# A scan traced in sixteen steps with three pieces of the q, k and v projections each, its dependent products queued behind a piece, and state buffers for each direction

## The chip, the core and the metric

The kernel runs on one core of a Trainium2 chip. A core has a matrix engine (TensorE, PE in the profile), a vector engine (VectorE, DVE), an activation engine (ScalarE, ACT), a general engine (GpSimd, POOL) and a queue engine that issues most transfers (SyncE, SP). Each of them works through its own instructions in a fixed order and waits on semaphores for the others. The metric is the device time of one execution in microseconds (us), taken as the median of several runs.

## The reference

One layer of a hybrid encoder on 1024 tokens of width 1024, in float32. What matters here is its first half:

```python
h = rmsnorm(x, norm_mix_w)
z, xbc, dt_raw, q, k, v = jnp.split(h @ w_in, offs, axis=-1)
y_ssm = ssd_mixer(z, xbc, dt_raw, ...)
y_na = neighbourhood_attention(q, k, v, ...)
x = x + jnp.concatenate([y_ssm, y_na], axis=-1) @ w_out
h = rmsnorm(x, norm_mlp_w)
return x + jnp.square(jax.nn.relu(h @ w_mlp_in)) @ w_mlp_out
```

`ssd_mixer` is a scan with a state, run forward and backward over 8 chunks of 128 tokens, for 2 groups of 8 heads with 64 columns each. In each direction a chunk needs the state that the chunk before it left:

```python
cb = jnp.einsum("bclgn,bcsgn->bclsg", cc, bc)
y_diag = jnp.einsum("bclsge,bcsgep->bclgep", cb[..., None] * decay, xc)
chunk_states = jnp.einsum("bclgn,bclgep->bcgepn", bc, xc * decay_to_end[..., None])
def step(h, inp):
    s_c, d_c = inp
    return d_c[..., None, None] * h + s_c, h
y_off = jnp.einsum("bclgn,bcgepn->bclgep", cc, h_in) * jnp.exp(a_cum)[..., None]
```

The two directions are added, gated with SiLU(z), normalised in groups of 512 columns and handed to the output projection together with the attention's result.

## The kernel before

Every large product is made of float32 split into a high and a low part: `mm3` (L177 to L180) issues three products for each step of the contraction. The low part of a weight (tile wl) is what VectorE or GpSimd subtracts from the raw load (wraw), the high part (wh) is copied by ScalarE (L148, L149).

The program runs in stages: the norm and transposes of h (to about 50 us), the projections to x, B, C with the convolution and to z (to 264.8 us), then the scan together with the projections to q, k and v (264.8 to 671.2 us), attention with a part of the output projection, the rest of the output projection, and the two layers of the MLP. The change rewrites the scan and its projections.

A scheduler orders the instructions of each engine before the program runs: it simulates the engines by a model of its own and gives each engine, of what is ready, what was traced first. The order in which the source issues things is thus a priority, and where instructions end up is seen in the built program only.

Names of the scan, for direction d, chunk c and group g (a chunk's 128 tokens by 512 columns):

- xs: the inputs, loaded from DRAM (L585 backward, L670 forward). xw: xs weighted for the state (L653, L672), split into xh and xl (L540, L541).
- `decay_state`: pS is the chunk's part of the state (product L541 and following by `mm3`), st the running state (L546, L549, L550), sh and sl its split (L553, L554). The buffer of sh and sl is one for each group, shared by both directions.
- `carried`: py is the part of the output that the carried state makes (`mm3` with sh, sl as its operands), yo the scaled py (L567); ch, cl is the split of C (L562, L563).
- `backward` also makes the part within the chunk, for both directions together: pcb is B times C (L587), rb the decay weights (two loads of 512 KB, L605; GpSimd subtracts, L612; VectorE's predicated copy, L618; the exponential, L623; times pcb, L625), pd the product of rb and xs (L630, eight products), y1 the sum (L638 to L642). The forward output of the first half of the chunks and the backward output of the second half go to DRAM (y1_dr) and are fetched again by the other direction (L648, L665).
- `gated`: times SiLU(z) (tile sz), the norm, and the store to y_dr (L579), on the queue of ScalarE.
- PSUM: pcb, pS and py take turns in two buffers (`ps_s`), the transposes ptq in two (`ps_tp`), pd has its own, the projections pq have others.

The scan's loop runs over the chunks and groups, 16 steps, and calls backward(7 - i, g) and forward(i, g). After it the projections are traced: for each of two halves of the columns q, then k, then v, each in 8 pieces. A piece is 128 tokens by 512 columns, 24 products pq, and what follows it (norm, transposes ptq, split hl, store). There are 48 pieces. Being traced after the scan they have the lower priority and fill the holes that the scan leaves on TensorE.

Behind that stage stand attention (L852 and following: loads of q, k, kl and v for a pair of heads, the mask nam, L786, the bias braw, L876, their sum mb on GpSimd, L881, scores psc, L931 and L934, their row maximum with the masked scores pr, L939, transposes ptp, L962) and the output projection that fills its holes (yl: loads of the gated scan output, L798; pty: its transposes, L807; po: its products; x: the residual, L830).

Of the kernel before, what the change touches and what calls it, by code (L numbers as in the profile page):

```python
# [9 lines left out]
F32 = mybir.dt.float32  # L10
F32R = mybir.dt.float32r
# [7 lines left out]
P = 128  # L19
# [36 lines left out]
def hymba_block(  # L56
# [162 lines left out]
    with ExitStack() as ph:  # L219
# [298 lines left out]
        with ExitStack() as p2:  # L518
# [15 lines left out]

            def decay_state(d, c, g, xw):
                prev = st[d][g]
                pS = ps_s("pS")
                xh = qp.tile([P, 512], F32R, tag="xh", name="xh", bufs=1)
                xl = qp.tile([P, 512], F32R, tag="xl", name="xl", bufs=1)
                nc.scalar.activation(xh, xw, AF.Copy)  # L540
                nc.vector.tensor_tensor(xl, xw, xh.bitcast(F32), op=sub)  # L541
                mm3(pS, bNh[:, c, g, :], bNl[:, c, g, :], xh, xl, True, True)
                new = prev and prev[0]
                if prev is None:
                    new = qp.tile([P, 512], F32, tag=f"st{d}{g}", name="st", bufs=1)
                    nc.vector.tensor_copy(new, pS)  # L546
                else:
                    dec = ed[:, d, c, 8 * g : 8 * g + 8]
                    nc.gpsimd.tensor_tensor(h8(new), h8(new), hb(dec), op=mul)  # L549
                    nc.vector.tensor_tensor(new, new, pS, op=add)  # L550
# [3 lines left out]
                nc.vector.tensor_tensor(sl, new, sh.bitcast(F32), op=sub)  # L554
                st[d][g] = (new, sh, sl)
# [24 lines left out]

            def backward(c, g):
                hs = slice(8 * g, 8 * g + 8)
                cs = slice(c * P, (c + 1) * P)
                xs = qp.tile([P, 512], F32, tag="xs", name="xs")
                nc.sync.dma_start(xs, xs_dr[c, :, g * 512 : (g + 1) * 512])  # L585
                pcb = ps_s("pcb")
                nc.tensor.matmul(  # L587
                    pcb[:, 0:P], lhsT=bT[:, g, cs], rhs=cT[:, g, cs], start=True, stop=True
                )
                cb = pcb[:, 0:P]  # L590
                jk = pcb[:, P : 2 * P]
                cd = qp.tile([P, 1], F32, tag="cd", name="cd")
                nc.vector.scalar_tensor_tensor(
                    jk, cb, 1.0, ident, op0=mul, op1=mul, accum_out=cd
                )
                cf = qp.tile([P, 8], F32, tag="cf", name="cf")
                nc.vector.scalar_tensor_tensor(
                    cf, dt[:, 1, c, hs], cd, dsk[:, hs], op0=mul, op1=add
                )
                pd = ps_v("pd")  # L600
                for q in range(2):
# [9 lines left out]
                    for d in range(2):  # L611
# [11 lines left out]
                    nc.scalar.activation(rb[:, 0], rb[:, 0], AF.Exp)  # L623
                    gm = rb[:, 0]
                    nc.vector.tensor_tensor(  # L625
                        gm, rb[:, 0], cb.unsqueeze(1).broadcast_to([P, 4, P]), op=mul
                    )
                    for j in range(4):
                        e = 4 * q + j
                        nc.tensor.matmul(  # L630
                            pd[:, e * HD : (e + 1) * HD],
                            lhsT=gm[:, j, :],
                            rhs=xs[:, e * HD : (e + 1) * HD],
                            start=True,
                            stop=True,
                        )
                y1 = qp.tile([P, 512], F32, tag="y1", name="y1")
                nc.gpsimd.tensor_tensor(h8(y1), h8(xs), hb(cf), op=mul)  # L638
                if c < NT - 1:
                    yo = carried(1, c, g)  # L640
                    nc.gpsimd.tensor_tensor(y1, y1, yo, op=add)
                nc.vector.tensor_tensor(y1, y1, pd, op=add)  # L642
                if c >= NT // 2:
                    nc.scalar.dma_start(y1_dr[c, :, g * 512 : (g + 1) * 512], y1)
                else:
# [4 lines left out]
                    gated(y1, c, g)  # L650
                if c > 0:
                    xw = qp.tile([P, 512], F32, tag="xw", name="xw", bufs=1)
                    nc.gpsimd.tensor_tensor(h8(xw), h8(xs), hb(wd[:, 1, c, hs]), op=mul)  # L653
                    decay_state(1, c, g, xw)

            def forward(c, g):
                hs = slice(8 * g, 8 * g + 8)
# [10 lines left out]
                if c < NT - 1:  # L668
                    xs = qp.tile([P, 512], F32, tag="xs", name="xs")
                    nc.sync.dma_start(xs, xs_dr[c, :, gs])  # L670
                    xw = qp.tile([P, 512], F32, tag="xw", name="xw", bufs=1)
                    nc.gpsimd.tensor_tensor(h8(xw), h8(xs), hb(wd[:, 0, c, hs]), op=mul)  # L672
                    decay_state(0, c, g, xw)
# [35 lines left out]

            for g in range(2):  # L710
                ps4 = slice(4 * g, 4 * g + 4)
                for b, pt, rt in qkv_proj(OFF_Q, g):
                    hl = normed_split(pt, rt, pcol[:, 80:81])
                    s = slice(b * P, (b + 1) * P)
                    for j in range(2):
                        for a in range(2):
                            nc.scalar.dma_start(
                                q_dr[ps4, 2 * j + (a ^ j), :, s].rearrange("p d t -> d p t"),
                                hl[j * HD : (j + 1) * HD, a],
                            )  # L720
                for b, pt, rt in qkv_proj(OFF_K, g):
                    hl = normed_split(pt, rt, pcol[:, 81:82])
                    nc.scalar.dma_start(
                        k_dr[g, :, :, :, b * P : (b + 1) * P].rearrange(
                            "a p f t -> f (a p) t"
                        ),
                        hl.rearrange("f a p t -> f (a p) t"),
                    )
                for b, pt, rt in qkv_proj(OFF_V, g):
                    hl = hp.tile([P, 8, 2, HD], F32R, tag="hl", name="hl", bufs=2)  # L730
                    split_from_psum(hl[:, :, 0], hl[:, :, 1], h8(pt), rt)
                    nc.scalar.dma_start(v_dr[b, :, 8 * g : 8 * g + 8], hl.bitcast(F32))

# [655 lines left out]
```

## Time and profile before

| | us |
|---|---|
| three runs, median | 1681.8 |
| lowest and highest | 1676.36 and 1685.55 |
| span of the profiled execution | 1676.4 |
| scan with the q, k and v projections | 264.8 to 671.2 |

The profiled execution's span agrees with the fastest run. The time outside the span is not seen apart in this profile. An engine's busy time in the page is a sum of the lengths of its instructions; those of TensorE overlap. "PE pcb L587 <- DVE yo L567: 6.7, 4, 2.6" reads: TensorE stood before the product pcb of line 587, and what it waited for last was VectorE's instruction that makes yo at line 567; 6.7 us in total, in 4 waits, the longest 2.6 us. In a row of the timeline the first number is the start in us from the span's start, the second the length, and the brackets hold the idle time before it with its releaser.

### The profile page before, as it was taken

The page shows a single profiled execution, that of the slowest core. Times are in us where ns is not written, and L with a number is a line of the kernel's source. Part 1 is how long each engine was busy: PE and PEld are TensorE (multiplying, and loading weights), DVE is VectorE, ACT ScalarE, POOL GpSimd, SP SyncE. Part 2 cuts the span into 40 slices and gives each one's busy share as a digit, 9 for nine tenths or more (in the row PEclk, how much of TensorE's full clock was granted, in tenths as well). Part 3 has the DMA queues.
Part 4 walks back from the last instruction along what each step waited for, and adds up shares of the span by engine and source line. Part 5 has one row for each costly group of instructions (what it writes and reads, how often), then busy time and mean ns, then how long its engine had stood idle before and what let it go on. Part 6 is the DMA issues. An engine that isn't in the chain of part 4 may idle for free. (4 is left out here: it accounts for less than half of the span.)

```text
span 1676.4 us, 20931 instructions
## 1 busy us (share of the span) xinstructions
PE 1590.8 (95%) x7453; PEld 1297.3 (77%) x7453; DVE 1106.0 (66%) x1686; ACT 721.3 (43%) x1187; POOL 708.4 (42%) x506
## 2 busy tenths in 40 slices
PE   6999999998988899998999989999999989999999
PEld 5788888777766678887778767788888868888887
DVE  5767214788796852888898867544243387887863
ACT  5434223434343442556565533554444444433330
POOL 4000003888687862322243232244444465455551
PEclk9999999999999999999999999999999989999999
DMA  8113337876666785956664141353344386644231
GB/s 217 51 38 105 93 100 212 215 194 196 229 220 173 218 263 190 281 165 185 180 190 118 62 164 50 101 201 126 138 164 150 127 295 231 216 149 151 101 101 75
DMA packets 178755, 269.75 MB, mean 161 GB/s; under 512 B 14219, under 2 KB 105307, under 8 KB 178651
## 3 DMA queue, kind: packets, MB, share of 16 engines
q1 hardware_dynamic: 134667, 227.51, 44.1%
q10 hardware_dynamic: 42976, 37.23, 7.3%
q0 software_dynamic: 1008, 3.67, 0.5%
q8 instruction: 59, 0.97, 0.3%
q14 instruction: 45, 0.37, 0.1%
HBM read 185.21 MB, written 86.50 MB: 162 GB/s over the span
## 5 line engine op out<-in xcount | busy, mean ns | idle before, releaser
L760 POOL TENSOR_TENSOR wl<-wraw,wh 128x1024 fp32r<-128x1024 f32 x110 | 298.5, 2724 | 318.4 <-ACT wh L759 297.1
L759 ACT ACTIVATE wh<-wraw 128x1024 fp32r<-128x1024 f32 x110 | 115.6, 1054 | 149.7 <-PE px L745 50.8
L745 PE MATMUL px<-wh,ahl 128*128 128x512 f32 x512 | 162.5, 395 | 3.3 <-ACT ahl L759 3.3
L179 PE MATMUL pq<-wl,hTh 128*128 128x512 f32 x384 | 153.6, 402 | 4.9 <-DVE wl L149 4.8
L178 PE MATMUL pq<-wh,hTh 128*128 128x512 f32 x384 | 154.4, 405 | 3.5 <-ACT wh L148 3.5
L745 PE MATMUL px<-h,wh 128*128 128x512 f32 x496 | 156.0, 396 | 1.4 <-DVE x L1078 1.4
L180 PE MATMUL pq<-wh,hTl 128*128 128x512 f32 x384 | 152.9, 399 | 0.0
L760 DVE TENSOR_TENSOR ahl<-ar,ahl 128x1024 fp32r<-128x1024 f32 x56 | 115.1, 2062 | 23.2 <-ACT ahl L759 22.1
L759 ACT ACTIVATE ahl<-ar 128x1024 fp32r<-128x1024 f32 x56 | 58.2, 1052 | 140.1 <-PE px L745 75.3
L745 PEld LDWEIGHTS px<-wh,ahl 128*128 128x128 f32 x512 | 97.0, 190 | 25.0 <-ACT ahl L759 3.7
L745 PEld LDWEIGHTS px<-h,wh 128*128 128x128 f32 x496 | 93.2, 188 | 24.0 <-ACT h L184 1.6
L149 DVE TENSOR_TENSOR wl<-wraw,wh 128x1024 fp32r<-128x1024 f32 x40 | 55.3, 1386 | 81.9 <-ACT wh L148 81.2
L745 PE MATMUL px<-wl,ahl 128*128 128x512 f32 x256 | 101.0, 395 | 0.0
L745 PE MATMUL px<-h,wl 128*128 128x512 f32 x248 | 98.1, 395 | 0.0
L881 POOL TENSOR_TENSOR mb<-braw,nam 128x256 f32<-128x256 f32 (+1 forms) x48 | 40.1, 863 | 131.1 <-DVE nmx L939 72.2
L179 PEld LDWEIGHTS pq<-wl,hTh 128*128 128x128 f32 x384 | 73.6, 192 | 23.1 <-DVE wl L149 8.6
L149 POOL TENSOR_TENSOR wl<-wraw,wh 128x1024 fp32r<-128x1024 f32 x18 | 43.0, 2401 | 110.5 <-ACT wh L148 110.5
L178 PEld LDWEIGHTS pq<-wh,hTh 128*128 128x128 f32 x384 | 74.0, 193 | 20.2 <-ACT wh L148 5.2
L184 ACT ACTIVATE pth<-ptp 128x384 fp32r<-128x384 f32 (+1 forms) x128 | 57.7, 455 | 73.1 <-PE ptp L962 72.5
L612 POOL TENSOR_TENSOR rb<-rb,c 128x512 f32<-128x512 f32 x64 | 77.0, 1223 | 20.4 <-DMA rb<-cum_dr 19.2
L180 PEld LDWEIGHTS pq<-wh,hTl 128*128 128x128 f32 x384 | 73.5, 191 | 15.0
L745 PE MATMUL pz<-h,wh 128*128 128x512 f32 x256 | 80.8, 396 | 0.8 <-DVE h L185 0.8
(268 smaller groups left out, 4211.4 us busy)
## 6 DMA issues: line engine op xcount, KB each, us to landing
ar<-act_dr SPq DMA_DIRECT2D x56, 512.0 KB, 3.7
act_dr<-cq SPq DMA_DIRECT2D x49, 512.0 KB, 3.2
wraw<-in_w_in_dram SPq DMA_DIRECT2D x44, 512.0 KB, 4.3
rb<-cum_dr SPq DMA_DIRECT2D x32, 512.0 KB, 7.2
wraw<-in_w_mlp_in_dram SPq DMA_DIRECT2D x32, 512.0 KB, 4.6
wraw<-in_w_mlp_out_dram SPq DMA_DIRECT2D x32, 512.0 KB, 5.2
q_dr<-hl ACTq DMA_DIRECT2D x64, 128.0 KB, 3.6
k_dr<-hl ACTq DMA_DIRECT2D x16, 512.0 KB, 5.3
```

Source lines behind the costliest of these rows:

```text
L149: lo_eng.tensor_tensor(lo[:, 0:n], raw[:, 0:n], hi[:, 0:n].bitcast(F32), op=sub)
L178: nc.tensor.matmul(pt, lhsT=ah, rhs=bh, start=first, stop=False)
L179: nc.tensor.matmul(pt, lhsT=ah, rhs=bl, start=False, stop=False)
L180: return nc.tensor.matmul(pt, lhsT=al, rhs=bh, start=False, stop=last)
L184: nc.scalar.activation(hi, src, AF.Copy)
L612: nc.gpsimd.tensor_tensor(rb[:, d], rb[:, d], c1[:, d, c, h0 : h0 + 4].unsqueeze(2).broadcast_to([P, 4, P]), op=sub,)
L745: nc.tensor.matmul(pt, lhsT=a, rhs=b, start=f, stop=l, skip_group_check=True)
L759: nc.scalar.activation(hl[0], src, AF.Copy)
L760: eng.tensor_tensor(hl[1], src, hl[0].bitcast(F32), op=sub)
L881: nc.gpsimd.tensor_tensor(mb[:, s].rearrange("p (s r c) -> p s r c", r=16, c=8), v[:, a:b], nam[:, s].rearrange("p (s r c) -> p s r c", r= ...
```

## The change

The scan's step is taken apart. `weights(c, g)` does all that does not need this step's projections: the loads, the chain of rb as far as the product with pcb, pcb, and the carried output of the backward direction. Then the next piece of the projections is traced; `mark` is its last product. Then follow `backward`, whose state product pS and whose pd are put behind `mark` on TensorE (`tc.issue_after(mark)`), `forward` with the same mark for its pS, and two more pieces. One piece stands ahead of the loop. So each of the 16 steps has three pieces, in place of projections that are traced after the whole scan.

pcb moves from the two buffers that it shared with pS and py to the two of the transposes. xh and xl get two buffers each. sh and sl get a buffer for each direction and group. `dynamic_dma_scratch_size=4096` is set for the program, and the memory that this frees holds the additional buffers.

```diff
-            def decay_state(d, c, g, xw):
+            def decay_state(d, c, g, xw, mark):
                 prev = st[d][g]
                 pS = ps_s("pS")
-                xh = qp.tile([P, 512], F32R, tag="xh", name="xh", bufs=1)
-                xl = qp.tile([P, 512], F32R, tag="xl", name="xl", bufs=1)
+                xh = qp.tile([P, 512], F32R, tag="xh", name="xh", bufs=2)
+                xl = qp.tile([P, 512], F32R, tag="xl", name="xl", bufs=2)
...
-                mm3(pS, bNh[:, c, g, :], bNl[:, c, g, :], xh, xl, True, True)
+                with tc.issue_after(mark):
+                    mm3(pS, bNh[:, c, g, :], bNl[:, c, g, :], xh, xl, True, True)
...
-                sh = qp.tile([P, 512], F32R, tag=f"sh{g}", name="sh", bufs=1)
-                sl = qp.tile([P, 512], F32R, tag=f"sl{g}", name="sl", bufs=1)
+                sh = qp.tile([P, 512], F32R, tag=f"sh{d}{g}", name="sh", bufs=1)
+                sl = qp.tile([P, 512], F32R, tag=f"sl{d}{g}", name="sl", bufs=1)
...
-            def backward(c, g):
+            def weights(c, g):
...
-                pcb = ps_s("pcb")
...
+                    rbs.append(rb)
+                pcb = ps_tp("pcb")
...
+                for rb in rbs:
                     nc.vector.tensor_tensor(
...
+                if c < NT - 1:
+                    yo = carried(1, c, g)
+                    nc.gpsimd.tensor_tensor(y1, y1, yo, op=add)
+                return xs, rbs, y1
+
+            def backward(c, g, xs, rbs, y1, mark):
+                hs = slice(8 * g, 8 * g + 8)
+                if c > 0:
+                    xw = qp.tile([P, 512], F32, tag="xw", name="xw", bufs=1)
+                    nc.gpsimd.tensor_tensor(h8(xw), h8(xs), hb(wd[:, 1, c, hs]), op=mul)
+                    decay_state(1, c, g, xw, mark)
+                pd = ps_v("pd")
+                with tc.issue_after(mark):
+                    for e in range(8):
                         nc.tensor.matmul(
...
-            for i in range(NT):
-                for g in range(2):
-                    backward(NT - 1 - i, g)
-                    forward(i, g)
...
-                        mm3(pt, hTh[s], hTl[s], *get(k), k == 0, k == KD - 1)
-                    yield b, pt, rcol[:, b : b + 1]
+                        mark = mm3(pt, hTh[s], hTl[s], *get(k), k == 0, k == KD - 1)
+                    yield b, pt, rcol[:, b : b + 1], mark.ins
...
+            units = qkv_units()
+            mark = next(units)
+            for n in range(2 * NT):
+                c, g = n // 2, n % 2
+                held = weights(NT - 1 - c, g)
+                mark = next(units)
+                backward(NT - 1 - c, g, *held, mark)
+                forward(c, g, mark)
+                for _ in range(2):
+                    mark = next(units, mark)
+            for mark in units:
+                pass
...
+    nc = bacc.Bacc(
+        "TRN2", target_bir_lowering=False, num_devices=1, dynamic_dma_scratch_size=4096
+    )
```

`qkv_units` is the old loop over q, k and v with its stores, which now hands out its mark after each piece.

What this does to the order shows at three places. The first is TensorE in the middle of the scan. Before, pd, pS and py of a step stand in one block, and the projections' products behind and ahead of it:

```order
L178 MATMUL pq<-wh,hTh 128x512
L179 MATMUL pq<-wl,hTh 128x512
L630 MATMUL pd<-xs,rb 128x64 x8
L178 MATMUL pS<-xh,bNh 128x512
L179 MATMUL pS<-xl,bNh 128x512
L180 MATMUL pS<-xh,bNl 128x512
L178 MATMUL py<-sh,ch 128x512
L179 MATMUL py<-sl,ch 128x512
L180 MATMUL py<-sh,cl 128x512
L705 MATMUL ptq<-ident,qn 128x128 x8
L180 MATMUL pq<-wh,hTl 128x512
L178 MATMUL pq<-wh,hTh 128x512
```

In the changed program one step's pS and py are still neighbours, but pd stands apart, a few products of a piece behind them (line 646 is pd's, line 178 to 180 are the three products of `mm3`):

```order
L179 MATMUL pS<-xl,bNh 128x512
L180 MATMUL pS<-xh,bNl 128x512
L178 MATMUL py<-sh,ch 128x512
L179 MATMUL py<-sl,ch 128x512
L180 MATMUL py<-sh,cl 128x512
L178 MATMUL pq<-wh,hTh 128x512
L179 MATMUL pq<-wl,hTh 128x512
L180 MATMUL pq<-wh,hTl 128x512
L178 MATMUL pq<-wh,hTh 128x512
L179 MATMUL pq<-wl,hTh 128x512
L180 MATMUL pq<-wh,hTl 128x512
L646 MATMUL pd<-xs,rb 128x64 x4
```

So the dependent products come in smaller groups with pieces between; the step's pcb stands 40 rows ahead of that pd, with a whole piece in between.

The second place is TensorE at the end of the stage. Before, the first scores of attention stand among the products of the projections, with some 190 of these still to come:

```order
L178 MATMUL pq<-wh,hTh 128x512
L179 MATMUL pq<-wl,hTh 128x512
L180 MATMUL pq<-wh,hTl 128x512
L931 MATMUL psc<-k,q 128x256
L934 MATMUL psc<-kl,q 128x256
L178 MATMUL pq<-wh,hTh 128x512
L931 MATMUL psc<-k,q 128x384
L934 MATMUL psc<-kl,q 128x384
L179 MATMUL pq<-wl,hTh 128x512
```

In the changed program they stand behind the last projection product (the third row), and the transposes of the output projection's operand (pty) and its first products (po) follow:

```order
L178 MATMUL pq<-wh,hTh 128x512
L179 MATMUL pq<-wl,hTh 128x512
L180 MATMUL pq<-wh,hTl 128x512
L940 MATMUL psc<-k,q 128x256
L940 MATMUL psc<-k,q 128x384
L943 MATMUL psc<-kl,q 128x256
L943 MATMUL psc<-kl,q 128x384
L816 MATMUL pty<-ident,yl 128x128 x8
L178 MATMUL po<-wh,yh 128x512
L179 MATMUL po<-wl,yh 128x512
L178 MATMUL po<-wh,yh 128x512
L179 MATMUL po<-wl,yh 128x512
```

What moved is the scan's end towards the projections' end: in the changed order the last py of the scan has 24 projection products behind it, and the last pd 19.

The third place is the queue of SP there, which issues loads in order. Before (y is the last fetch of y1_dr, then the loads for the first pair of heads, the mask, the gated scan output and the bias; the residual x comes twelve issues later):

```order
L665 DMA y_3415<-y_dr 128x512
L852 DMA q<-q_dr 128x2x1024
L855 DMA k<-k_dr 64x2x1024 x2
L866 DMA kl<-k_dr 64x1024 x2
L868 DMA v<-v_dr 128x8x256
L786 DMA nam<-namask_dram 128x896
L798 DMA yl<-y_dr 128x8x128 x4
L876 DMA braw<-t_dr 128x384
```

In the changed program:

```order
L672 DMA y_5386<-y_dr 128x512
L861 DMA q<-q_dr 128x2x1024
L864 DMA k<-k_dr 64x2x1024 x2
L875 DMA kl<-k_dr 64x1024 x2
L877 DMA v<-v_dr 128x8x256
L147 DMA wraw<-in_w_out_dram 128x2x512 x2
L839 DMA x_5441<-in_x_dram 128x512 x7
L795 DMA nam<-namask_dram 128x896
L807 DMA yl<-y_dr 128x8x128 x4
L885 DMA braw<-t_dr 128x384
```

The loads of x, which take the memory of h and so wait for the last projection product, have moved ahead of nam, yl and braw.

More of the change, by code (lines that the diff above doesn't have):

```diff
@@ L585, in backward @@
                 nc.sync.dma_start(xs, xs_dr[c, :, g * 512 : (g + 1) * 512])
-                pcb = ps_s("pcb")
[L587 to L600, printed above, removed]
+                rbs = []
                 for q in range(2):
@@ L623, in backward @@
                     nc.scalar.activation(rb[:, 0], rb[:, 0], AF.Exp)
-                    gm = rb[:, 0]
+                    rbs.append(rb)
+                pcb = ps_tp("pcb")
+                nc.tensor.matmul(
+                    pcb[:, 0:P], lhsT=bT[:, g, cs], rhs=cT[:, g, cs], start=True, stop=True
+                )
+                cb = pcb[:, 0:P]
+                jk = pcb[:, P : 2 * P]
+                cd = qp.tile([P, 1], F32, tag="cd", name="cd")
+                nc.vector.scalar_tensor_tensor(
+                    jk, cb, 1.0, ident, op0=mul, op1=mul, accum_out=cd
+                )
+                cf = qp.tile([P, 8], F32, tag="cf", name="cf")
+                nc.vector.scalar_tensor_tensor(
+                    cf, dt[:, 1, c, hs], cd, dsk[:, hs], op0=mul, op1=add
+                )
+                y1 = qp.tile([P, 512], F32, tag="y1", name="y1")
+                nc.gpsimd.tensor_tensor(h8(y1), h8(xs), hb(cf), op=mul)
+                for rb in rbs:
                     nc.vector.tensor_tensor(
-                        gm, rb[:, 0], cb.unsqueeze(1).broadcast_to([P, 4, P]), op=mul
+                        rb[:, 0], rb[:, 0], cb.unsqueeze(1).broadcast_to([P, 4, P]), op=mul
                     )
-                    for j in range(4):
-                        e = 4 * q + j
+                if c < NT - 1:
[11 more added lines that the diff above has]
+                    for e in range(8):
                         nc.tensor.matmul(
                             pd[:, e * HD : (e + 1) * HD],
-                            lhsT=gm[:, j, :],
+                            lhsT=rbs[e // 4][:, 0, e % 4, :],
                             rhs=xs[:, e * HD : (e + 1) * HD],
@@ L708, in normed_split @@
                 return hl.bitcast(F32).rearrange("f a (p t) -> f a p t", p=4)
[L710 to L732, printed above, removed]
@@ new lines, in qkv_units @@
+            def qkv_units():
+                for g in range(2):
+                    ps4 = slice(4 * g, 4 * g + 4)
+                    for b, pt, rt, mark in qkv_proj(OFF_Q, g):
+                        hl = normed_split(pt, rt, pcol[:, 80:81])
+                        s = slice(b * P, (b + 1) * P)
+                        for j in range(2):
+                            for a in range(2):
+                                nc.scalar.dma_start(
+                                    q_dr[ps4, 2 * j + (a ^ j), :, s].rearrange("p d t -> d p t"),
+                                    hl[j * HD : (j + 1) * HD, a],
+                                )
+                        yield mark
+                    for b, pt, rt, mark in qkv_proj(OFF_K, g):
+                        hl = normed_split(pt, rt, pcol[:, 81:82])
+                        nc.scalar.dma_start(
+                            k_dr[g, :, :, :, b * P : (b + 1) * P].rearrange(
+                                "a p f t -> f (a p) t"
+                            ),
+                            hl.rearrange("f a p t -> f (a p) t"),
+                        )
+                        yield mark
+                    for b, pt, rt, mark in qkv_proj(OFF_V, g):
+                        hl = hp.tile([P, 8, 2, HD], F32R, tag="hl", name="hl", bufs=2)
+                        split_from_psum(hl[:, :, 0], hl[:, :, 1], h8(pt), rt)
+                        nc.scalar.dma_start(v_dr[b, :, 8 * g : 8 * g + 8], hl.bitcast(F32))
+                        yield mark
```

15 lines of the change are left out of this document (3 added, 12 removed).

## The prediction

> **What bounds the kernel now.** I read the page first, then the windows of the stage that the change rewrites (264.8 to 671.2 us, from the first to the last product of the q, k and v projections), then the waits of TensorE there, then single rows.
>
> ```profile
> PE 1590.8 (95%) x7453; PEld 1297.3 (77%) x7453; DVE 1106.0 (66%) x1686; ACT 721.3 (43%) x1187; POOL 708.4 (42%) x506
> 264.80:671.20 406.40, 371.29 (x1748) 297.62 (x1747) 290.87 (x419) 155.09 (x270) 285.39 (x266) 0.97 0.74 216
> 280.00:600.00 320.00, 287.23 (x1371) 228.73 (x1370) 258.91 (x375) 128.03 (x230) 253.97 (x235) 0.97 0.73 208
> 540.00:550.00 10.00, 5.95 (x21) 4.38 (x22) 8.06 (x13) 3.19 (x6) 9.84 (x9) 0.83 0.54 130
> 560.00:570.00 10.00, 7.89 (x31) 4.69 (x29) 9.55 (x10) 5.48 (x9) 8.87 (x7) 1.00 0.88 246
> 650.00:660.00 10.00, 10.00 (x46) 8.29 (x45) 1.50 (x2) 0.96 (x2) 0.00 (x0) 1.00 0.27 107
> ```
>
> Columns of the last five are the length, busy time of PE, PEld, DVE, ACT and POOL, the granted clock, the DMA share and GB/s. PE bounds the whole kernel, but this stage has two faces. While the scan runs (280 to 600) VectorE is busy 81% (258.91 of 320) and GpSimd 79% (253.97), and PE has holes. From about 600 on PE runs projection products alone, without a hole, and the vector engines idle. Those products start 0.23 us apart though each counts as 0.39 busy:
>
> ```profile
> L178 PE MATMUL pq<-wh,hTh x384: 387/389/775, 264.8 to 670.5; 128*128 128x512 f32 x192
> 670.69 0.39 PE L179 MATMUL pq<-wl,hTh 128*128 128x512 f32 x1
> 670.92 0.40 PE L180 MATMUL pq<-wh,hTl 128*128 128x512 f32 x1
> ```
>
> There are 3 x 384 = 1152 of them, 1152 x 0.23 = 265 us of the 406; one piece (24 products) is 5.5 us. The waits of PE between 270 and 700:
>
> ```profile
> PE pd L630 <- DVE rb L625: 6.9, 7, 1.6
> PE pcb L587 <- DVE yo L567: 6.7, 4, 2.6
> PE pq L179 <- DVE wl L149: 4.8, 7, 1.3
> PE pq L178 <- ACT wh L148: 3.5, 4, 1.9
> PE pcb L587 <- DVE st L550: 3.3, 1, 3.3
> PE pd L630 <- issue: 2.2, 1, 2.2
> PE py L179 <- DVE sl L554: 2.1, 3, 1.2
> PE py L178 <- DVE st L550: 1.9, 3, 1.4
> PE py L178 <- DVE yo L567: 1.1, 2, 0.6
> PE pS L178 <- ACT rb L623: 0.8, 1, 0.8
> PE ptq L705 <- ACT sz L576: 0.8, 1, 0.8
> PE ptq L705 <- DVE qn L699: 0.5, 2, 0.3
> ```
>
> They sum to 34.6 us. Beside them stands the clock: at a mean of 0.97, 3% of 406 us is 12.2 us. Its drops follow the longer waits:
>
> ```profile
> 543.22 0.80 PE L587 MATMUL pcb<-cT,bT 128*128 128x128 f32 x2 [3.32 <-DVE st L550]
> 545.95 0.59 PE L180 MATMUL pq<-wh,hTl 128*128 128x512 f32 x1
> 546.37 0.39 PE L178 MATMUL pq<-wh,hTh 128*128 128x512 f32 x1
> ```
>
> After a wait of 3.32 us the products come 0.42 us apart until 546.37, where they are 0.39 long again, and that window (540 to 550) shows 0.83. So 46.8 us of the stage are loss, and this is all that the change can win, because the products on PE are the same before and after.
>
> **The change, term by term.**
>
> *pcb.* 6.7 + 3.3 = 10.0 us. The product of B and C waits because its PSUM buffer is one of the two that pS and py also use, so it waits for whoever reads those. In the changed kernel it takes a buffer of the pool of the transposes ptq, whose own waits are the 0.8 and 0.5 above. I keep 1 and win 9.
>
> *pd.* 6.9 + 2.2 = 9.1 us. The weights rb of pd come down a chain:
>
> ```profile
> rb<-cum_dr SPq DMA_DIRECT2D x32, 512.0 KB, 7.2
> L612 POOL TENSOR_TENSOR rb<-rb,c 128x512 f32<-128x512 f32 x61 | 73.0, 1217 | 19.8 <-DMA rb<-cum_dr 18.6 <-PE pq L180 1.0
> L618 DVE COPY_PREDICATED rb<-lmask,rb 128x512 f32<-128x512 int32 x31 | 40.6, 1309 | 15.3 <-POOL rb L612 15.1
> L625 DVE TENSOR_TENSOR rb<-rb,pcb 128x512 f32<-128x512 f32 x32 | 21.2, 678 | 4.3 <-ACT rb L623 4.2
> ```
>
> 7.2 for the load, 2 x 1.22, 2 x 1.31 and 2 x 0.68 make 13.6 us, without the exponential and without queueing. The loss can fall because the whole chain is now traced ahead of a piece of 5.5 us and pd behind it, and a step has (406.4 - 46.8)/16 = 22 us of PE work. It does not fall to nothing: rb still has two buffers, so the next load waits for this pd; in the order three steps hold only about 14 us of PE work from pd to pd. At about 1 us for each of the three I keep 3 and win 6.1.
>
> *py.* 2.1 + 1.9 + 1.1 = 5.1 us. sh and sl get a buffer for each direction, so one direction's split no longer waits for the other's py. But py stands right behind pS at many places still (second fence of the order). I keep 2 and win 3.1.
>
> *wl, wh.* 4.8 + 3.5 = 8.3 us. Weight splits share VectorE and ScalarE with the scan. Spread evenly, that load is 290.87 us over some 372 instead of 258.91 over 320, 78% instead of 81%, hardly less: I keep 4 and win 4.3. *pS and ptq:* 2.1, keep 1, win 1.1.
>
> Together the waits win 23.6. *Clock:* nearly all waits of 2 us and more are those of pcb and the one issue, so I keep 2 of 12.2 and win 10.2. The longest wait in the list is 3.3 us, and a drop of the clock stands behind it. [...]
>
> The scan stage thus ends **34 us** earlier, at about 637 us. The bounds are 0 (every wait only changes its name) and 46.8.
>
> *The end of the stage.* This is where the change costs. Call E the end of the last projection product. Before, the last scan product on PE was over some 70 us ahead of E, and all that attention and the output projection need was made ready beneath the pure products:
>
> ```profile
> L179 PE MATMUL py<-sl,ch x28: 389/393/632, 312.3 to 594.0; 128*128 128x512 f32 x28
> 612.45 0.34 ACTq L579 DMA_DIRECT2D y_dr<-y  x1
> 614.97 0.35 SPq L786 DMA_DIRECT2D nam<-namask_dram  x1
> 616.38 8.74 SPq L798 DMA_DIRECT2D yl<-y_dr  x4
> 625.16 3.14 SPq L876 DMA_DIRECT2D braw<-t_dr  x1
> 634.52 2.41 POOL L881 TENSOR_TENSOR mb<-braw,nam 128x384 f32<-128x384 f32 x3 [3.74 <-issue]
> 673.73 5.25 SPq L830 DMA_DIRECT2D x<-in_x_dram  x7
> 674.06 0.41 DVE L939 CUSTOM_DVE_ANT_0 pr<-psc,mb 128x256 f32<-128x256 f32 x1
> L962 PE MATMUL ptp<-ident,pr x352: 270/272/447, 681.5 to 962.7; 128*128 128x128 f32 x176
> ```
>
> From the last py (594.2 with its 0.2) to the last gated store is 18.2 us; nam, which is queued on SP behind it, goes 2.5 later; the first ptp comes 7.4 us behind the first pr, 10.3 behind E. In the changed order only one piece stands behind the last py, so py ends at E - 6 and the store leaves at E + 12. nam waits for that store to land, yl and braw are queued behind nam on SP, so nam goes at E + 15. Five bare issues of about 0.35 put braw at E + 17; with the 1.4 + 8.8 of the rows it is E + 25.
>
> ```profile
> braw<-t_dr SPq DMA_DIRECT2D x16, 192.0 KB, 5.0
> yl<-y_dr SPq DMA_DIRECT2D x8, 512.0 KB, 8.5
> ```
>
> braw lands at E + 22 (or 30); mb 0.8, pr 0.4 and 7.4 more give the first ptp at E + 31 (or 39) against 10.3. PE meanwhile has four psc, then pty, which needs yl: at E + 24 by 8.5 us from E + 15.5. Both say 21 to 24 us without work on PE, or 29 by the slower issue. The seven loads of x now stand ahead of nam on SP and wait for E (they reuse the memory of hTh and hTl); at 5.25 us of issue, as in the row, they are done before the store lands, so they add nothing. I take **22 us**, nearest to the bare issues, because q, k and v are no longer issued right ahead of yl. Bounds: 12, if the chain from py to the store takes half of its 18.2 us without the projections' work in GpSimd's queue, and 33, if all 40.3 us from the last py to mb (594.2 to 634.5) recur behind E - 6. After such a hole the clock is half for a while; the drop above lasted from 543.2 to 546.4, so half of these 3.2 us, **1.6 us**, is added.
>
> *The DMA scratch* of 4096 bytes gives memory back for the doubled buffers. What could feel it are the stores that GpSimd issues later:
>
> ```profile
> act_dr<-cq POOLq DMA_DIRECT2D x7, 512.0 KB, 10.2
> ```
>
> If some had to wait for each other the bound is four times 10.2, 41 us; I take 0, since no group on the page waits for act_dr from GpSimd. The doubled xh and xl take away a wait that no PE row shows: 0.
>
> **Sum.** -23.6 - 10.2 + 22 + 1.6 = -10.2 us. The profiled execution spans 1676.4 us, which equals the fastest of the three runs and is 5.4 below the median of 1681.8. So the span would be 1666.2, and a median of runs **1672**.
>
> **Rivals.**
>
> 1. *The hole at E eats the gain.* If yl and braw are issued as slowly as before, E costs 31 instead of 24, and with a gain of 31 to 34 the time is 1679 to 1682, no change. For it speaks that the issue rows are measured; against it that they were behind q, k and v.
>
> 2. *The scan runs without loss.* If kept waits are 3 instead of 11, clock included, and the chain at E is near its lower bound, -44 + 14 + 2 = -28: 1654. For it: a step has 22 us of PE work against a chain of 14. Against it: VectorE and GpSimd stay 4/5 busy, and an order fixed beforehand meets other delays than it was made for.
>
> 3. *The clock stays low.* Short waits stay spread over the whole stage instead of ending at 600, and the granted clock keeps 0.97: the 10.2 are lost, -23.6 + 23.6 = 0, 1682. The rows speak against it: 560 to 570 has 2.1 us of holes at a clock of 1.00, only the single long wait of 540 to 550 brings 0.83. [...]
>
> 4. *Slower: the loop from pd through rb to the next pd sets the step.* rb has two buffers; the next load waits for pd, and pd now also waits for a whole piece in PE's fixed order. If GpSimd and VectorE, 79 and 81% busy, take some 8 us of queueing beside the 13.6, a step is as long as PE's 22 and pd waits in most of them. With 1.5 us lost in each of 16 steps on top of the 11 kept, the gain is 34 - 24 = 10, the hole costs 23.6, and the time is 1695. It decides as soon as the gain is below 15 us, that is, when more than 31 of the 46.8 stay.
>
> **How the numbers follow.** Forecast 0.45, rivals 1 to 4: 0.14, 0.17, 0.06, 0.15, the scratch 0.03. 0.5% (8.4 us) is about what a measurement can tell from no change: below 1673.4 is faster, above 1690.2 slower. Of the forecast (1664 to 1680 by the bounds of its terms that are not extreme) 0.33 lies in faster and 0.12 in the same; rival 2 is faster, 1 and 3 the same, 4 and the scratch slower: 0.50, 0.32, 0.18. The range 1653 to 1695 reaches from rival 2 to rival 4.
>
> **What would show it.** Right: pcb gone from PE's waits, pd under 4 us in all, no clock under 0.9 in the scan, the last projection product near 637 us, and right behind it a hole of about 20 us that ends with pty, while SP issues nam about 15 us after E. Wrong: the last product after 655 us with pd or py leading the waits (rival 4), a hole under 12 us (rival 2), or stores by GpSimd far longer than 10.2 us.

## The result, and the profile after

The changed kernel takes 1709.26 us (median of 4 runs, 1703.94 to 1711.09), the kernel before in the same comparison 1682.1 us. The ratio is 1.0161, 95% interval 1.0136 to 1.0186: slower by 1.6%. Forecast were 1672 us and a gain. The profiled execution spans 1709.3 us against 1676.4, 32.9 us more, and this is what is taken apart below. The medians lie 27.2 us apart: the profiled execution of after is its longest (1711.09 us), that of before agrees with its shortest, so some 6 us of the 32.9 are spread between executions.

The page's totals, the window of the stage that was rewritten, and the tiles whose first and last rows mark the stage's borders:

```profile
PE 1595.5 (93%) x7453; PEld 1303.9 (76%) x7453; DVE 1093.7 (64%) x1686; ACT 722.9 (42%) x1187; POOL 704.7 (41%) x506
267.40:661.50 394.10, 365.23 (x1737) 296.90 (x1735) 275.03 (x415) 151.00 (x262) 270.63 (x251) 0.97 0.68 205
661.50:699.00 37.50, 10.86 (x46) 8.16 (x46) 6.60 (x13) 8.82 (x17) 15.81 (x15) 0.64 1.06 308
L178 PE MATMUL pq<-wh,hTh x384: 387/389/774, 267.4 to 660.9; 128*128 128x512 f32 x192
L180 PE MATMUL pq<-wh,hTl x384: 387/389/632, 268.1 to 661.3; 128*128 128x512 f32 x192
L178 PE MATMUL py<-sh,ch x28: 387/467/764, 319.5 to 652.5; 128*128 128x512 f32 x28
L971 PE MATMUL ptp<-ident,pr x352: 270/272/329, 703.1 to 994.2; 128*128 128x128 f32 x176
L178 PE MATMUL po<-wh,hl x32: 388/394/792, 998.9 to 1050.1; 128*128 128x512 f32 x32
```

The work of each engine is within about 1% of what it was. The stage is shorter (394 instead of 406 us) at the same clock of 0.97. Directly behind it lies a stretch of 37.5 us in which TensorE is busy for 10.9 and the transfer engines are full (a share of 1.06 at 308 GB/s). The waits of TensorE from 267 to 730 us (us in total, times, longest) say what stands in it:

```profile
PE pty L816 <- DMA yl<-y_dr: 16.1, 1, 16.1
PE psc L940 <- DMA k<-k_dr: 9.7, 1, 9.7
PE pq L179 <- DVE wl L149: 9.0, 7, 4.2
PE psc L940 <- DVE nmx L948: 6.0, 2, 5.6
PE pS L178 <- ACT xh L540: 5.8, 5, 2.0
PE py L178 <- ACT sz L577: 4.7, 2, 3.2
PE pd L646 <- DVE rb L629: 3.9, 3, 1.6
PE py L178 <- DVE yo L568: 2.1, 4, 1.0
PE ptq L703 <- DVE qn L697: 1.9, 3, 1.2
```

The first two are one hole at the hand-over to attention, 25.8 us, and pcb is gone from the list. But pS, py, wl and ptq wait longer than before (the prediction shows the list of before). The balance in four stretches of the two profiled executions, with the first row of "po<-wh,hl", the output projection's last part, as the mark behind attention (967.4 us in the execution of before, whose last projection product began at 670.9):

| stretch | before, us | after, us | difference |
|---|---|---|---|
| to the first projection product | 264.8 | 267.4 | +2.6 |
| from there to the last one | 406.1 | 393.9 | -12.2 |
| hand-over and attention, to the last part of the output projection | 296.5 | 337.6 | +41.1 |
| from there to the end | 709.0 | 710.4 | +1.4 |

The loads of SP at the hand-over, from the timeline (start, length, queue, line):

```profile
658.98 1.29 SPq L864 DMA_DIRECT2D k<-k_dr  x2
672.71 9.59 SPq L839 DMA_DIRECT2D x<-in_x_dram  x7
682.34 0.43 SPq L795 DMA_DIRECT2D nam<-namask_dram  x1
682.81 6.65 SPq L807 DMA_DIRECT2D yl<-y_dr  x4
695.08 16.99 SPq L839 DMA_DIRECT2D x<-in_x_dram  x9
713.83 0.33 SPq L885 DMA_DIRECT2D braw<-t_dr  x1
723.84 0.69 PE L940 MATMUL psc<-k,q 128*128 128x384 f32 x1 [5.64 <-DVE nmx L948]
```

k is loaded only 2.3 us ahead of the last projection product, nam goes 21 us behind it. The second bias (braw) stands behind nine more loads of x, and the scores wait once more for it, 5.64 us.

### The profile page after: what moved, and what is told of

Its sections match the earlier page's. It is cut to its first block, busy times and chain, and to the rows that moved or that the text cites. A ratio compares the mean times of both kernels' runs of the same rounds, so it can differ in the third digit from the quotient of the medians.

```text
span 1709.3 us, 20877 instructions
## 1 busy us (share of the span) xinstructions
PE 1595.5 (93%) x7453; PEld 1303.9 (76%) x7453; DVE 1093.7 (64%) x1686; ACT 722.9 (42%) x1187; POOL 704.7 (41%) x506
## 5 line engine op out<-in xcount | busy, mean ns | idle before, releaser
L769 POOL TENSOR_TENSOR wl<-wraw,wh 128x1024 fp32r<-128x1024 f32 x110 | 297.5, 2715 | 320.7 <-ACT wh L768 300.5
L179 PEld LDWEIGHTS pq<-wl,hTh 128*128 128x128 f32 x384 | 73.3, 191 | 27.6 <-DVE wl L149 12.8
L599 POOL TENSOR_TENSOR rb<-rb,c 128x512 f32<-128x512 f32 x64 | 69.8, 1111 | 38.8 <-DMA rb<-cum_dr 37.5
L958 ACT ACTIVATE pr<-pr,nmx 128x384 f32<-128x384 f32 (+1 forms) x128 | 74.9, 586 | 24.7 <-DVE nmx L948 23.6
```

What stands on the lines that cost most here:

```text
L179: nc.tensor.matmul(pt, lhsT=ah, rhs=bl, start=False, stop=False)
L599: nc.gpsimd.tensor_tensor(rb[:, d], rb[:, d], c1[:, d, c, h0 : h0 + 4].unsqueeze(2).broadcast_to([P, 4, P]), op=sub,)
L769: eng.tensor_tensor(hl[1], src, hl[0].bitcast(F32), op=sub)
L958: nc.scalar.activation(pr[:, 0:n], pr[:, 0:n], AF.Exp, bias=nmx[:, b : b + 1], scale=-1.0, accum_out=db,)
```

## The experiments

Each was run next to the kernel before; a ratio is to the kernel before, with its 95% interval. "Stage" is from the first to the last projection product, as in the second row of the table.

**Two pieces in a step.** The first question was whether the loss lies where the scan ends or in what the scan's steps have become.

```diff
-                for _ in range(2):
+                for _ in range(1):
                     mark = next(units, mark)
```

> Two pieces of the projections in each step instead of three (one ahead of pd and pS, one behind); the other 15 of the 48 pieces follow after the scan. Theory A (the loss lies in the hand-over: the scan's last outputs become ready at the same time as the last projection product, so the loads for attention and the output projection come too late): the hole of 26 us on TensorE behind the last projection product goes, first ptp about 10 us behind that product instead of 41, time 1665 to 1680. Theory B (the loss is made by the smaller DMA scratch or by the split of the steps, wherever the scan ends): the hole or an equal loss stays, 1695 or more.

1690.95 us, ratio 1.0057 (1.0031 to 1.0082). The waits between 255 and 800 us have no load in them any more, and the rows of the stage's end and the first ptp are:

```profile
L180 PE MATMUL pq<-wh,hTl x384: 387/389/774, 267.6 to 678.4; 128*128 128x512 f32 x192
L178 PE MATMUL py<-sh,ch x28: 389/472/792, 313.5 to 601.6; 128*128 128x512 f32 x28
L971 PE MATMUL ptp<-ident,pr x352: 270/272/421, 689.1 to 971.9; 128*128 128x128 f32 x176
```

The hole is gone, as theory A has it: the last py stands 77 us ahead of the last projection product and ptp 10.7 behind it (41.8 in the changed kernel). The time is above theory A's 1665 to 1680. Of the 10.8 us by which the profiled execution (1687.2) is longer than that of before, 5.4 stand in the stage, which takes 411.5 us; the rest is spread over the other three stretches, about 2 us in each.

**All but the loop.** The kernel before with pcb's new pool, the doubled and separated buffers and the scratch:

> The kernel before with all of the change but the new loop: pcb in the pool of the transposes, two xh and xl, sh and sl for each direction, scratch 4096. Theory A: no hole at the hand-over, the waits of pcb (10.0 us) mostly go, 1665 to 1677. Theory B (scratch): 1690 or more, with a longer first stage and slower loads.

1795.5 us, ratio 1.069 (1.0655 to 1.0725). This was far outside theory A. It is taken apart by the next three.

**State buffers alone** (`sh{d}{g}`, `sl{d}{g}`, two xh and xl, scratch 4096, on the kernel before):

> The kernel before with the state buffers alone: sh and sl for each direction, two xh and xl, scratch 4096; pcb stays in its old pool. Theory D (pcb in the pool of the transposes is what cost the old loop 115 us): 1665 to 1685. Theory E (the state buffers are, because pS, py and pd get another order by them): 1750 or more.

1692.23 us, ratio 1.007 (1.0048 to 1.0093).

**pcb's pool alone**, one line of the kernel before:

```diff
-                pcb = ps_s("pcb")
+                pcb = ps_tp("pcb")
```

> The kernel before with pcb in the pool of the transposes and nothing else. Theory D: 1750 or more. Theory E: pcb's waits of 10.0 us mostly go, 1665 to 1680.

1810.28 us, ratio 1.0771 (1.0713 to 1.0828): theory D. The windows of the projections' products alone (length, busy time of PE, clock, transfers), first of this run, then of the kernel before, show where it goes:

```profile
320.00:520.00 200.00, 0.00 (x0) 0.56 0.50 145
520.00:600.00 80.00, 56.50 (x222) 0.89 0.76 221
```

```profile
320.00:520.00 200.00, 131.61 (x513) 0.98 0.70 205
```

For 200 us not one projection product runs beside the scan, and the clock falls to 0.56. No transpose ptq runs there either (0.00 busy, x0, in the same window). That pcb, traced earlier, takes the two buffers that the transposes of the projections need, so that a piece cannot be finished and the next not begun, is the reading that fits, and is not shown; that this one line costs the time is shown.

**The scratch alone**, the order of all engines unchanged:

> The kernel before with the DMA scratch of 4096 bytes and nothing else; each engine's order is the same. The prediction's term of 0: within 0.3% of the kernel before. Theory B: slower by more than 0.5%, in the first stage or in the MLP where GpSimd issues stores.

1682.5 us, ratio 1.0019 (1.0 to 1.0039). The term of 0 holds within 0.4%. Its stage begins at 266.2 us, against 264.8, with the same order, so 1.4 of the 2.6 us in the table's first row appear without any change of order. Its stage takes 403.7 us against 406.1, and its hand-over and attention 3.0 us more: differences of 2 to 3 us between two profiled executions need no cause in the order.

**Without the marks** (both `with tc.issue_after(mark)` left out):

> The changed kernel without the two marks, so pS and pd may be ordered ahead of the piece. Theory A: within 8 us of the changed kernel's 1709, since the hand-over stays as it is. Rival C (the marks make TensorE wait in the scan: pS on xh 5.8 us, py 6.8 us): the last projection product comes more than 10 us before the changed kernel's 661, time under 1700.

1708.37 us, ratio 1.0175 (1.0134 to 1.0217), stage 394.6. No help and no cost of the marks can be seen: rival C falls.

**pcb back in its old pool, in the new loop** (`pcb = ps_s("pcb")`):

> The changed kernel with pcb back in the two buffers of pS and py. If the prediction's term of 9 us for pcb holds in the new loop, waits of pcb of 5 to 10 us come back and the last projection product comes 5 to 12 us after the changed kernel's 661. If the new loop leaves those buffers free anyway, it is within 3 us.

1702.84 us, ratio 1.0142 (1.0097 to 1.0188). The waits of this run have no row of pcb, and its stage is 392.1 us:

```profile
PE ptq L703 <- DVE qn L697: 14.7, 8, 4.9
PE pq L179 <- DVE wl L149: 3.8, 4, 1.4
PE py L178 <- ACT sz L577: 3.0, 1, 3.0
L180 PE MATMUL pq<-wh,hTl x384: 387/390/629, 269.0 to 660.4; 128*128 128x512 f32 x192
```

So in the new loop pcb's pool isn't worth 9 us, but nothing or less. The waits of ptq grow by 12.8 us, others shrink, and the stage stays. The time, from two runs, has an interval that overlaps that of the changed kernel.

**The queue of SP at the hand-over.** First the loads of x alone were put behind yl:

```diff
-                    nc.sync.dma_start(
+                    yld = nc.sync.dma_start(
...
+                    with tc.issue_after(yld.ins):
                         nc.sync.dma_start(
```

> The changed kernel with the loads of x for the output projection queued on SP behind nam and yl. Theory A: nam goes about 13 us behind the last projection product instead of 21, pty starts about 8 us earlier, 1699 to 1703. If yl is bound by the store's landing or by bandwidth and not by the queue, under 3 us are won: 1706 to 1709.

1711.94 us, ratio 1.0199 (1.017 to 1.0228). This told nothing on the question: a later weight load took the place of x in the queue and went only at 685.0 us, and nam at 685.4, 22 behind the last projection product. In a second attempt the later weight loads and those of the norm's weights were put there too:

> The changed kernel with the loads of x, the later weight loads of the output projection and the norm's weights all queued on SP behind nam and yl, which the earlier attempt did not reach. If the queue sets the hole: nam goes 13 to 15 us behind the last projection product instead of 21, pty starts 6 to 8 us earlier, 1700 to 1704. If bandwidth or the store sets it: pty within 2 us of its time in the changed kernel, 1707 to 1711.

1704.6 us, ratio 1.015 (1.0115 to 1.0184), against 1709.26 for the changed kernel. The two intervals overlap, so the gain is read from the hand-over and not from the time. The last two rows are from the timeline of ScalarE's queue and from SP's waits:

```profile
669.61 0.35 SPq L795 DMA_DIRECT2D nam<-namask_dram  x1
672.00 10.58 SPq L809 DMA_DIRECT2D yl<-y_dr  x4
672.12 0.87 PE L944 MATMUL psc<-k,q 128*128 128x256 f32 x2 [9.17 <-DMA k<-k_dr]
682.74 1.97 PE L818 MATMUL pty<-ident,yl 128*128 128x128 f32 x8 [8.49 <-DMA yl<-y_dr]
673.43 0.94 ACTq L580 DMA_DIRECT2D y_dr<-y  x2
SPq L795 <- DMA k<-k_dr: 6.0, 1, 6.0
```

The last projection product began at 662.6, so nam goes 7 us behind it and pty 20 (28 in the changed kernel). The queue set 8 us of the hole; 17.7 of its 25.8 stay, the wait for k among them hardly changed.

The row of ScalarE's queue shows one thing more. The last two gated stores went at 673.43 us, behind nam (669.61) and behind the first load of yl (672.00). So neither waits for the last gated store: the first four loads of yl read the columns of group 0 (`f` from 0 to 3), and the last two stores are the last step's, of group 1. What nam waited for on SP was the landing of k, 6.0 us; in the kernel before it was kl, 8.4 us.

**How much lead the hand-over needs.** Two and three pieces in turn (`1 + n % 2` pieces behind the mark), or three in the first eight steps and two in the last eight (`2 if n < 8 else 1`); both leave 7 pieces to be traced after the loop:

> The changed kernel with two and three pieces in turn in a step, so that 7 of the 48 pieces (39 us of products) follow after the scan. Theory A: the hand-over needs some 31 us more lead than the changed kernel gives it, so no hole is left (under 5 us), the stage of the scan is between 394 us (three pieces) and 412 us (two), time 1673 to 1683. If the hole stays over 10 us, the loads there are slow by themselves and not late.

> The changed kernel with three pieces in each of the first eight steps and two in each of the last eight, so that 7 pieces (39 us of products) follow after the scan. Theory A: no hole at the hand-over (under 5 us), as with 7 pieces left by turns. If the steps of three pieces are what makes the scan's stage short (394 us with three, 412 with two, 417 by turns), the stage is 395 to 408 us and the time 1670 to 1684; if the stage depends on the order by chance more than on the number, 408 to 418 us and 1685 to 1697.

1696.9 us, ratio 1.0096 (1.0067 to 1.0124), and 1698.52 us, ratio 1.0111 (1.0075 to 1.0146). The pieces left over are no measure of the lead, because the scheduler drew them into the scan in the second case; the distance in the profile is. The second run's last long wait, and the rows that give its lead:

```profile
PE pty L816 <- DMA yl<-y_dr: 10.0, 1, 10.0
L178 PE MATMUL py<-sh,ch x28: 387/396/792, 317.3 to 650.6; 128*128 128x512 f32 x28
L180 PE MATMUL pq<-wh,hTl x384: 386/390/632, 268.0 to 673.6; 128*128 128x512 f32 x192
```

| kernel | last py to last projection product | stage | hand-over and attention, against before |
|---|---|---|---|
| before | 77.8 | 406.1 | 0 |
| changed | 8.8 | 393.9 | +41.1 |
| three pieces, then two | 23.0 | 406.3 | +19.8 |
| two and three in turn | 64.3 | 417.8 | +2.6 |
| two in a step | 76.8 | 411.5 | +1.7 |

All in us, from the profiled executions. The cost follows the lead. The other runs with the new loop agree: with 6 to 14 us of lead it lies between +33.6 and +39.9 (in no order within them), with 72 us at +4.9 and +6.3. By the 3.0 us of the scratch run, the last two entries of the table can't be told from 0. The stage's length does not follow the number of pieces by any rule that these runs show: turns took 417.8 us, longer than both pure forms, so the expectations' "394 with three, 412 with two" explains nothing by itself. The granted clock goes along with it: from 280 to 600 us it is 0.97 before and in the changed kernel, and 0.95 with two in a step and with two and three in turn, and two hundredths of these 320 us are some 6 us (an estimate, as if TensorE had been busy throughout).

**What holds the stage up.** Two kernels leave work out of the chain of rb: the predicated copies on VectorE (with a scale in the exponential in place of the mask), or one of the two subtractions on GpSimd.

> The changed kernel without the predicated copies of rb on VectorE (32 times 1.31 us, left out; the exponential takes a scale instead of the mask). Theory F (the scan's stage is held up by the queues of VectorE and GpSimd, in which small steps of the recurrence stand behind the rb chain): the stage, 394 us in the changed kernel, falls by more than 10 us. Rival G (the loss belongs to the recurrence itself: the hand-over from pS to the state and back to py in each step, whatever else those queues hold): within 5 us.

> The changed kernel with one of the two subtractions on each rb left out on GpSimd (32 times 1.2 us). Theory F: the stage falls by more than 8 us from 394. Rival G: within 5 us.

One run each: 1705.08 us with a stage of 391.9, and 1693.44 us with a stage of 384.4:

```profile
L178 PE MATMUL pq<-wh,hTh x384: 387/389/776, 266.0 to 649.9; 128*128 128x512 f32 x192
L180 PE MATMUL pq<-wh,hTl x384: 387/389/628, 266.7 to 650.4; 128*128 128x512 f32 x192
```

Less work on VectorE moves the stage by 2 us, less on GpSimd by 9.5: theory F for GpSimd, not for VectorE. Both edits also shorten the chain of rb, by 1.3 and 1.2 us an instruction, so the difference between them speaks for GpSimd's load and against the chain's length. The scheduler orders both kernels anew, and 2 us is no more than the stage of the scratch run differed by with an unchanged order, so the sizes are rough.

**Versions that might beat both.** Two pieces and pcb's old pool together, and then with one subtraction of each rb moved to ScalarE; last, that move alone on the kernel before:

```diff
-                    for d in range(2):
-                        nc.gpsimd.tensor_tensor(
-                            rb[:, d],
-                            rb[:, d],
-                            c1[:, d, c, h0 : h0 + 4].unsqueeze(2).broadcast_to([P, 4, P]),
-                            op=sub,
-                        )
+                    nc.gpsimd.tensor_tensor(
+                        rb[:, 0],
+                        c1[:, 0, c, h0 : h0 + 4].unsqueeze(2).broadcast_to([P, 4, P]),
+                        rb[:, 0],
+                        op=sub,
+                    )
+                    for j in range(4):
+                        nc.scalar.activation(
+                            rb[:, 1, j, :],
+                            rb[:, 1, j, :],
+                            AF.Identity,
+                            scale=-1.0,
+                            bias=c1[:, 1, c, h0 + j : h0 + j + 1],
+                        )
...
-                    nc.scalar.activation(rb[:, 0], rb[:, 0], AF.Exp)
+                    nc.scalar.activation(rb[:, 0], rb[:, 0], AF.Exp, scale=-1.0)
```

> Two pieces in a step, and pcb back in the two buffers of pS and py: the two edits that were each faster than the changed kernel (1691 and 1703 against 1709). If they add, 1680 to 1687, about the kernel before. If the stage with two pieces stays at 412 us, 1688 to 1694.

> Two pieces a step with pcb in its old pool, and one of the two subtractions on each rb done by ScalarE (four activations with a bias) in place of GpSimd, the same arithmetic. If GpSimd's queue is a bound of the scan's stage (leaving that subtraction out took 9.5 us off), the stage falls from 406 by 4 to 10 us: 1671 to 1678, below the kernel before. If ScalarE's queue takes its place, within 3 us of 1682.

> The kernel before with the same subtraction moved to ScalarE and nothing else. If GpSimd's queue bounds its scan as well: stage 396 to 402 instead of 406, 1669 to 1675. If not, within 3 us of 1680.

The first takes 1682.29 us, ratio 1.0017 (0.9995 to 1.0038), so the two edits add and bring back what the change lost, no more. The second takes 1684.99 us, ratio 1.0025 (1.0007 to 1.0043), no gain, though its stage is 402.3 us against 406.2 in the first. The third takes 1673.23 us, ratio 0.9956 (0.9939 to 0.9974): it beats the kernel before, by 0.4%. Its stage and its greatest wait:

```profile
L178 PE MATMUL pq<-wh,hTh x384: 387/389/775, 267.2 to 666.3; 128*128 128x512 f32 x192
L180 PE MATMUL pq<-wh,hTl x384: 387/389/628, 267.9 to 666.8; 128*128 128x512 f32 x192
PE py L178 <- DVE st L550: 16.0, 8, 3.2
```

399.6 us instead of 406.1. Again the old waits shrank (pd and pcb had 19.1 us together and have 5.3), and again one wait stands in their place, now py on the state, the recurrence itself.

## Why the prediction was wrong

**The gain in the scan, forecast -34, measured -12.2.** This is the first term that failed. Of its parts:

- *pcb, 10.0 us, forecast to keep 1.* The waits of pcb did go. But the 9 us were not won by the pool, and the step that failed is that the new pool takes them out of the stage: with the old pool in the new loop pcb doesn't wait either, and the stage is no longer (392.1). The new pool alone costs some 130 us in the old loop (1810.28 against 1678.38 in the same comparison). That the transposes, whose waits were 1.3 us, would have room for pcb was read from their waits as they were, without pcb in their buffers.
- *pd, 9.1 us, forecast 3.* Measured 4.4 (3.9 and 0.5), near.
- *py, 5.1 us, forecast 2; pS and ptq, 2.1, forecast 1; wl and wh, 8.3, forecast 4.* Measured 6.8, 7.9 and 9.6 (with the small rows of each). All three grew. The waits of py on sl and st, 4.0 us, did go, but sz and yo stand in their place with 4.7 and 2.1. The step "sh and sl get a buffer for each direction, so one direction's split no longer waits for the other's py" took one cause of a wait for all its length; the state buffers alone (with the doubled xh and xl and the scratch) made the kernel slower by 0.7%.
- *The clock, 12.2 us, forecast 2.* The mean stayed at 0.97. Long waits of the new kinds stand in place of the old: 4.21 us before pq on wl, 3.19 before py. Rival 3 had the clock stay low, by many short waits; here a clock of 0.50 stands behind few: 2.04, 1.92, 4.21 and 3.19 us (windows 288 to 291, 414 to 420, 527 to 530 and 585 to 588). The waits of 2 us and more did go with pcb, but others of that length came.

The sum of the waits in the stage is 28.7 us against a forecast of 11 and 34.6 before. So 5.9 of the 12.2 us are waits. The rest is busy time of TensorE, 371.0 us before and 365.0 after; 2.5 of these 6.0 are four scores and nine rows of pty that stood inside the stage before and stand behind it now, which only moves them. For the rest no cause is shown. Rival 4 had priced a gain of 10, near the measured 12.2, but by pd and rb, and pd was not it. Its remark that GpSimd and VectorE are four fifths busy was the right place to look, on GpSimd's side: leaving out one of its subtractions took 9.5 us off the stage (one run), and moving that one in the kernel before gave the only gain against it. What the trace does not settle is how far each of the new waits comes from GpSimd's queue and how far from the recurrence.

**The hand-over, forecast +23.6 (22 and 1.6), measured +41.1.** The direction was right, and the lead's table shows it: with the scan's end next to the stage's end, the next stage stands without its loads. The path was wrong in its middle, and the size was off. The hole alone was 25.8 us, near the forecast of 22, which is partly luck, because it is made of other pieces: 9.7 before the scores on k and 16.1 before pty on yl. The bound of 33 was worked out for the first ptp, and held there (31.2); for what came behind it there was no term. The sub-steps that failed:

- *"nam waits for that store to land".* The forecast's path ran from the last py through the last gated store to nam and yl. The store went at E + 10 (the first row of the pair is at 671.48), near the forecast E + 12, but nothing in the hole waited for it: with the queue put in another order nam and the first yl went ahead of it. What nam and yl stood behind is SP's own queue, with the loads of weights and x ahead of them, and the landing of k, kl and v.
- *"q, k and v are no longer issued right ahead of yl", taken as already loaded.* They stand behind the fetch of y on SP, which waits for the scan, and went 2.3 us ahead of the last projection product; k cost 9.7 us.
- *The seven loads of x "add nothing".* They were to be done before the store landed. They began 11 us behind the last projection product, after two weight loads that waited 7.7 us for GpSimd, and took 9.6 us of issue instead of 5.25, ahead of nam; SP's waits before these loads are for v, kl and the weights to land (8.5 us). Putting them and the weights behind yl brought pty 8 us forward.
- *The first ptp "at E + 31 (or 39)".* It came 41.8 us behind the last projection product, against 10.6: 31.2 of the 41.1 have arisen by then.
- *Nothing was counted behind the first ptp.* The other 9.9 us lie there, among them 5.64 before psc, for a bias queued on SP behind nine loads of x.

**The other terms.** The scratch at 0: right within 0.4%; that GpSimd's later stores could feel it was the author's supposition, which no run shows. The doubled xh and xl at 0: not tried alone; with the separated states they are part of the 0.7%. The first stage's 2.6 us were not forecast; over all runs its length lies between 264.8 and 268.3 us, and no cause is shown.

**The sum.** -12.2 + 41.1 + 2.6 + 1.4 = +32.9 us, where -34 + 23.6 = -10.2 (rounded) was forecast. Both large terms failed to the same side, and the range's upper end held only one of them failing.

## What to carry to other kernels

Waits of a stage that is full on several engines are not a sum that an edit can take parts from (here 23.6 us of waits were to go, and 5.9 did): take one away and see which is late next, or test what the stage's length does when load, not a wait, is taken off an engine. When work that fills holes is spread evenly to the end of a stage, the last outputs of the dependent chain come at its end too (here the last py 8.8 us ahead of the last projection product, 77.8 before); count the lead that the next stage's loads need (here over 23 us; with 64 us and more it cost 1.7 to 6.3) and leave that much filling work behind the chain. Before a tile is moved to another pool, the waits of that pool's users say little on what it will cost there (here they were 1.3 us, and the move alone cost some 130).

## What the runs showed that was not expected

One line that moved a 128 x 128 product's PSUM tile to another pool of two buffers cost some 130 us (1810.28 against 1678.38), while no projection product ran for 200 us. Its granted clock was 0.56 in that stretch. In the timeline there, from 361.5 to 419.5 us, TensorE had the scan's products alone and sat idle for 22.8 of the 57.9 us.

The clock also drops behind shorter waits than the 3.3 us from which the forecast took its drop, and once for longer. In the changed kernel pS waited 1.92 us on xh, and the window behind it shows half the clock for 6 us in which TensorE was never idle. A wait of 1.94 us before a product on wl was followed by no drop (third and fourth row), so in these rows the length of a wait does not decide it alone:

```profile
413.53 0.50 PE L178 MATMUL pS<-xh,bNh 128*128 128x512 f32 x1 [1.92 <-ACT xh L540]
414.00:420.00 6.00, 6.00 (x24) 5.42 (x23) 6.00 (x9) 1.78 (x3) 4.72 (x4) 0.50 0.23 62
531.61 0.50 PE L179 MATMUL pq<-wl,hTh 128*128 128x512 f32 x1 [1.94 <-DVE wl L149]
530.00:540.00 10.00, 7.43 (x33) 5.62 (x34) 10.00 (x16) 6.25 (x11) 9.42 (x10) 1.00 0.69 210
690.00:694.00 4.00, 4.00 (x16) 3.18 (x16) 1.50 (x2) 1.37 (x2) 0.00 (x0) 0.52 1.20 295
```

The last row is what stands behind the two waits of 9.7 and 16.1 us at the hand-over. From 667 to 690 the granted clock is 0.50 as well, but TensorE is busy for only 2.0 us of that time. So the long hole slowed about 6 us of work, no more than the wait of 1.92 us did.
